# Modulation weights on another DMA queue, and scores of 512 queries in one bank: a diffusion layer on one core

## The chip, the core and the metric

The kernel runs on one core of one Trainium2 chip. Its engines work side by side, each through its own list of instructions in order: PE (TensorE, matmuls, with its weight loads shown as PEld), DVE (VectorE), ACT (ScalarE), POOL (GpSimd) and SP (SyncE). POOL and SP here do little but issue DMAs, each from a queue of its own. The metric is device time in microseconds of one execution, the median of three timed runs. Beside it stands one profiled execution, from which all durations of single instructions are taken.

## What is computed

One layer of a diffusion backbone in float32: 512 latent tokens and 256 context tokens of width 1024. Three parts follow each other: a SwiGLU network (FFN1), a pair of token mixers (retention and a convolution), and a second SwiGLU network. Each is modulated by vectors that come from a conditioning vector `c` times a large weight, `w_mod`.

```python
mods   = split(silu(c)     @ w_mod + b_mod, 9)          # shift, scale, gate for each of the three parts
mods_c = split(silu(c_ctx) @ w_mod + b_mod, 9)          # the same for the context tokens

h  = h  + 0.5 * g1  * swiglu(modulate(h,  n1, sh1,  sc1 ), w_ffn1_in, w_ffn1_out)
hc = hc + 0.5 * g1c * swiglu(modulate(hc, n1, sh1c, sc1c), w_ffn1_in, w_ffn1_out)

u, uc = modulate(h, nm, sh2, sc2), modulate(hc, nm, sh2c, sc2c)
q, k, v, rg, cv, ga, gb = split(u @ w_in)               # k and v of the context from uc
o = bidir_retention(rope(q), rope(k), v, decays, states of the context)     # 4 heads, 256 wide, values 512 wide
h = h + g2 * ((sigmoid(ga) * retention_branch(o, rg) + sigmoid(gb) * conv_branch(cv)) @ w_o)

h = h + 0.5 * g3 * swiglu(modulate(h, n2, sh3, sc3), w_ffn2_in, w_ffn2_out)
out = rmsnorm(h, final_norm)
```

For the retention, the kernel writes both directions and the context's state as one weighted product: the score of query n and key m is q.k times a decay that depends on n - m alone, over 512 latent and 256 context keys, and the output is the scores times the values.

## The kernel before

**Number format.** Each float32 operand of a matmul is split into a rounded high part and a low remainder (`split`, lines 320 and 321, or `unit`, lines 102 to 107: a DMA into `wraw`, the high part `wh` by ScalarE in line 104, the low part `wl` by VectorE in line 106). A product is then three matmuls (`mm3`, lines 113 to 115): high by high, high by low, low by high. The columns streamed by one matmul are at most 512, which fill one of the eight banks of the accumulator memory (`ps`, tag `ps`, 8 buffers).

**FFN1.** The 22 blocks of 128 hidden channels are worked off in six groups, `GROUPS1`. A group first forms its input products and then its output products. From the second group on, the input products of one block are a `chunk` (lines 414 to 470): seven block products in place of eight, each of 12 matmuls of 384 columns (line 439), with sums on VectorE before and after. A chunk loads two halves of `w1i` (lines 418 and 419, on SyncE) into `wraw`, which has four buffers: two chunks' worth. VectorE forms sums of the halves (425, 426, 429, 430), ScalarE and VectorE split them (393 and 394). Four accumulators are used for seven products: `pc` holds the fifth product, VectorE takes it off in line 453 (`p7 = p7 - pc`), and only then can the seventh product go into `pc`. So PE waits at that place for VectorE's line 453.

The output products of a group (`STEPS_OUT` loop) write partial sums to DRAM: `part_sum` scales the accumulator on ScalarE (666, 667) and adds it to `hdram` by an accumulating DMA that POOL issues (668).

**Modulation steps beside FFN1.** The later modulation vectors are formed while FFN1 runs, in 48 steps. A step (`mods`, lines 214 to 227) loads a 128x1024 block of `w_mod`, 512 KB, into a tile `wm`, of which there are two buffers (line 217), and multiplies and sums it on VectorE (226), once, or twice for vectors that the context needs too. So the load of step n must wait until the sum of step n - 2 has been taken. All 48 loads are issued by POOL (line 220). The steps are dealt out by `STEPS_OUT` = (8, 5, 5, 4, 4, 0) to the output products of the six groups and by `STEPS_IN` = (0, 5, 5, 4, 4, 4) to their input products, where `beside` calls `mod_step` (line 493). Counted from 0, steps 0 to 7 go with the first group's output products, 8 to 12 with the second group's input products, 13 to 17 with its output products, 18 to 22, 23 to 27, 28 to 31, 32 to 35, 36 to 39, 40 to 43 and 44 to 47 with the rest in turn. A step among output products also gets `past`, a column of the partial sum before: ScalarE copies it into the tile (line 219) ahead of the load, which keeps the load from going out before that partial sum is there.

**What sets the order.** The program is written as one sequence; a scheduler then lays out each engine's list ahead of time. At each point it takes, of the instructions that it expects to be able to run on that engine, the one that comes first in the program; what it expects comes from its own cost model. On the chip each list is run strictly in order, and an instruction that waits holds up all behind it on its engine or queue.

**Retention, one head** (`retention`, lines 811 to 967). Queries and keys are projected and rotated (`roped`), the context's keys projected (`keys_c`). Then, for two halves of 256 queries (`nh`, line 893): scores for three pairs of key blocks (each pair fills one bank with 2 x 256 columns, line 907), the decay by one VectorE product per pair (913, with the decays read from the strips `sx` and `sc` through `windows`, lines 786 to 789), a split (915) into tiles `gc0` to `gc5`. After the first half's scores come the values (`values`, 144 matmuls of 512 columns into six banks) and a convolution chunk, after the second half's scores the first two gates. Each half ends with the outputs of its two blocks of 128 queries (line 930, 18 matmuls each) and their normalisation (932 to 936).

Of the kernel before, what the change touches and what calls it, by code (L numbers as in the profile page):

```python
# [10 lines left out]
F32 = mybir.dt.float32  # L11
# [5 lines left out]
P = 128  # L17
# [47 lines left out]
def hybrid_layer_kernel(ctx: ExitStack, tc: tile.TileContext, a: dict, out: bass.AP):  # L65
# [23 lines left out]
    def ps(shape=(P, 512)):  # L89
        count[0] += 1  # L90
        return pp.tile(list(shape), F32, tag="ps", name=f"ps_{count[0]}")
# [119 lines left out]
        nc.vector.tensor_scalar(ab1[:, 1, b, v:v + 1], dots[:, b, v, 0:1], dots[:, b, v, 1:2],  # L211
                                vec[:, V_BM + b:V_BM + b + 1], ALU.add, ALU.add)

    def mods(n, past=None):

        i, b = MOD_STEPS[n]
        raw = t_((P, D), F32, "wm", 2)
        if past is not None:
            nc.scalar.copy(raw[:, 0:1], past)
        nc.gpsimd.dma_start(raw, a["w_mod"][n])  # L220
        j = 8 * i + b
        for v, dst in ((0, mx), (1, mc)):
            if v == 1 and i > 4:
                continue
            junk = tmp((P, D), BF16)
            nc.vector.scalar_tensor_tensor(  # L226
                junk, raw, 1.0, ccrow[v], ALU.mult, ALU.mult, accum_out=dst[:, j:j + 1])
# [244 lines left out]
    def ffn1(u):  # L472
        g = []

        def keep(j, s):
            hi, lo = t_((P, LA), F32R, f"hx{2 * j}"), t_((P, LA), F32R, f"hx{2 * j + 1}")
            split(hi, lo, s)
            g.append((hi, lo))

        def gate(s, c, pa, pb):  # L480
            nc.scalar.activation(s[:, c], pa, AF.Silu)
            nc.vector.tensor_mul(s[:, c], s[:, c], pb)

        ux, uc = part(u, xs), part(u, cx)
        todo_g = start(ux, uc, gate)

        nc.gpsimd.dma_start(hdram[:, 0, L - 1:L + 1], todo_g[0][:, L - 1:L + 1])
        nc.gpsimd.dma_start(hdram[:, :, xs], a["xT"])
        nc.gpsimd.dma_start(hdram[:, :, cx], a["ctxT"])
        off = 0  # L490
        for gi, (k0, nk) in enumerate(GROUPS1):
            steps = spread(STEPS_IN[gi], 2 * nk - 2)
            beside = lambda: mod_step(next(steps, 0))
            for j in range(2 if k0 == 0 else 0, nk):
                if k0 and j == nk - 1:
                    g.append((t_((P, LA), F32R, f"hx{2 * j}"), t_((P, LA), F32R, f"hx{2 * j + 1}")))
                    chunk(k0 + j, u, t, beside, lambda s, c: split(g[-1][0][:, c], g[-1][1][:, c], s[:, c]))
                elif k0:
                    keep(j, chunk(k0 + j, u, t, beside, None))
                    beside()  # L500
                if k0:
                    continue
                wa, wb = units(a["w1i"][j])
                pa, pb, pc = ps(), ps(), ps((P, 2, LC))
                proj(pa, wa, ux)
                proj(pb, wb, ux)
                proj(pc[:, 0, :], wa, uc)
                proj(pc[:, 1, :], wb, uc)
                if j == 2:
                    t = [operands(kb) for kb in range(4)]  # L510
                    for i, s in enumerate(todo_g):
                        keep(i, s)
                s = t_((P, LA), F32, "sg", 4)
                gate(s, xs, pa, pb)
                gate(s, cx, pc[:, 0, :], pc[:, 1, :])
                keep(j, s)
            n = 2 * nk * P
            last = k0 + nk == NJ
            gx_, gc_ = part(g, xs), part(g, cx)
            if last:  # L520
                h, hc = open_h()

            def out_units(mm):
                hi, lo = unit(a["w1o"][mm, :, off:off + n], n)
                return [(hi[:, i * n // 2:(i + 1) * n // 2], lo[:, i * n // 2:(i + 1) * n // 2]) for i in range(2)]

            steps = spread(STEPS_OUT[gi], 8)
            past = None
            for mm in () if last else range(4):
                w = out_units(mm)  # L530
                px, pc = [ps() for _ in range(2)], [ps() for _ in range(2)]
                for ks in (range(nk - 1), (nk - 1,)) if mm == 0 else (range(nk),):
                    for i in range(2):
                        proj(px[i], w[i], gx_, ks)
                        proj(pc[i][:, :LC], w[i], gc_, ks)
                for i in range(2):
                    mod_step(next(steps), past)
                    r = part_sum(2 * mm + i, px[i], pc[i][:, :LC])
                    past = r[:, 0:1] if k0 else None
            if last:  # L540

                w = [x for mm in range(4) for x in out_units(mm)]
                pc = [ps()[:, :LC] for _ in range(6)]
                for ks in (range(nk - 1), (nk - 1,)):
                    for i in range(6):
                        proj(pc[i], w[i], gc_, ks)
                        if ks[-1] == nk - 1:
                            evac1c(hc, i, pc[i])
                for i in (6, 7):
                    pc = ps()[:, :LC]  # L550
                    proj(pc, w[i], gc_)
                    evac1c(hc, i, pc)
                for i in range(4):
                    px = ps()
                    proj(px, w[i], gx_)
                    evac1(h, i, px, xs)
                    tail1(i - 4, h, hc)
                px = [ps() for _ in range(4)]
                for m, c in enumerate(HALVES):
                    for i in range(4):  # L560
                        proj(px[i][:, c], w[4 + i], gx_, c=c)
                        evac1(h, 4 + i, px[i][:, c], c)
                        tail1(4 * m + i, h, hc)
            off += n
            del g[:]
        return h
# [69 lines left out]
    def spread(total, slots):  # L636
        return (total * (i + 1) // slots - total * i // slots for i in range(slots))

    def mod_step(count, past=None):
        for _ in range(count):  # L640
            if todo:
                n = todo.pop(0)
                mods(n, past)
                if n < 8:
                    for key, src in (("x1", mx), ("c1", mc)):
                        nc.vector.tensor_scalar(hg[key][:, n:n + 1], src[:, 16 + n:17 + n],
# [136 lines left out]
        nc.vector.tensor_add(t1, t1, t2)  # L783
        split(hi, lo, t1)

    def windows(strip, off, n):

        w = strip[:, off:off + n]
        return bass.AP(w.tensor, w.offset, [list(w.ap[0]), [P, 2], [1, n]])

    def strips(hd):

        gf, gb = lg[:, hd:hd + 1], lg[:, 4 + hd:5 + hd]
# [17 lines left out]
    def retention(hd):  # L811
# [78 lines left out]
            gate.append((g, g[:, i % 2, :]))  # L890


        for nh in range(2):
            qs = slice(nh * 256, (nh + 1) * 256)
            pt = []
            for i in range(3):
                pq = ps((P, 2, 256))
                for jj in range(2):
                    mb = 2 * i + 1 - jj
                    for kb in range(2):  # L900
                        if mb < 4:
                            ks = slice(mb * P, (mb + 1) * P)
                            w = kh[:, kb, ks], kl[:, kb, ks]
                        else:
                            ks = slice((mb - 4) * P, (mb - 3) * P)
                            w = kch[:, kb, ks], kcl[:, kb, ks]
                        mm3(pq[:, jj, :], w, (q[kb][0][:, qs], q[kb][1][:, qs]), kb == 0, kb == 1)
                s = tmp((P, 2, 256))
                if i < 2:
                    dw = windows(sx, 384 - P * (2 * i + 1) + nh * 256, 256)  # L910
                else:
                    dw = windows(sc, nh * 256, 256)
                nc.vector.tensor_mul(s, pq, dw)
                hi, lo = t_((P, 2, 256), F32R, f"gc{i}"), t_((P, 2, 256), F32R, f"gc{3 + i}")
                split(hi, lo, s)
                pt.append((hi, lo))
            if nh == 0:
                values()
                conv_at(hd)
            else:  # L920
                wr = units(a["w_rg"][2 * hd])
                for i in range(2):
                    gates(i, wr[i])
            for nb in range(2):
                tb = 2 * nh + nb
                po = ps()
                for mb in range(6):
                    hi, lo = pt[mb // 2]
                    w = (hi[:, 1 - mb % 2, nb * P:(nb + 1) * P], lo[:, 1 - mb % 2, nb * P:(nb + 1) * P])
                    mm3(po, w, v[mb], mb == 0, mb == 5)  # L930
                bs = tmp((P, 16))
                nc.vector.bn_stats(bs[:, 0:6], po)
                nc.vector.bn_aggr(bs[:, 6:8], bs[:, 0:6])
                rsqrt(bs[:, 9:10], bs[:, 8:9], bs[:, 7:8], 1.0)
                o = t_((P, DV), F32, f"o{tb}")
                nc.vector.tensor_scalar(o, po, bs[:, 6:7], bs[:, 9:10], ALU.subtract, ALU.mult)
                on.append(o)
        r = []

        def gated(db):  # L940
# [267 lines left out]
```

## Time and profile before

| | |
|---|---|
| median of the timed runs | 1764.94 us |
| lowest and highest of three | 1762.32 and 1765.55 us |
| the profiled execution | 1768.33 us |
| its span | 1766.6 us |
| instructions | 22538 |
| granted TensorE clock over the span | 0.988 |
| loads of `wm` by POOL | 48, 512.0 KB each, 5.1 us to landing (median) |
| accumulating writes of `hdram` by POOL | 40, 384.0 KB each, 7.4 us |
| loads of `w1i` by SyncE | 44, 512.0 KB each, 4.8 us |

The span runs from the first to the last instruction; the profiled execution's own time is 1.7 us longer. In rows of the timeline the columns are start, duration, engine, line, operation, output and inputs with their shapes, and in brackets the idle time of the engine before it and what ended it. Matmuls overlap each other, so the distance from start to start tells what one costs, not its duration. A row of the waits names who waited for whom, then the sum in us, how many times, and the longest. A row of DMA issues gives the count, the size and the median time from issue to landing.

### The profile page before, as it was taken

What the parts mean: (1) busy time and instruction counts of PE and PEld (TensorE: products, weight loads), DVE (VectorE), ACT (ScalarE), POOL (GpSimd) and SP (SyncE); (2) the same over time, 40 slices, a digit from 0 to 9 for tenths busy, and PEclk for the clock granted to TensorE, in tenths of its full rate; (3) what the DMA queues carried; (4) which work ended last, traced back from release to release, by engine and by line L of the source; (5) the groups of instructions that cost most, each with busy time, mean ns of one, the idle gap of its engine ahead of it and who ended that gap; (6) DMA issues with size and microseconds to landing.
All of it is one profiled execution on the core that took longest, in us unless ns stands there. A gap on an engine that the chain in (4) does not pass through costs nothing. (4 is left out here: it accounts for less than half of the span.)

```text
span 1766.6 us, 22538 instructions
## 1 busy us (share of the span) xinstructions
PE 1724.1 (98%) x8947; PEld 1499.1 (85%) x8947; DVE 1146.1 (65%) x1831; ACT 672.1 (38%) x964; POOL 116.3 (7%) x208
## 2 busy tenths in 40 slices
PE   7899999998999999999999999999999999999997
PEld 4689999997999988888888888888888988888887
DVE  6895868575667898792985778393755644333335
ACT  4543444443434623342342433233563422222222
POOL 0011020201111100000000000001100000000000
PEclk9999999998999999999999999999999999999998
DMA  9267383847554321251151124215553244223221
GB/s 329 73 239 153 120 203 119 202 114 191 137 161 157 125 85 60 72 178 60 48 170 68 60 78 161 71 37 181 202 189 119 72 161 137 96 88 103 95 84 49
DMA packets 67999, 223.03 MB, mean 126 GB/s; under 512 B 8178, under 2 KB 9202, under 8 KB 67892
## 3 DMA queue, kind: packets, MB, share of 16 engines
q1 hardware_dynamic: 44928, 146.82, 24.8%
q0 software_dynamic: 22240, 73.69, 15.0%
q8 instruction: 70, 1.15, 0.3%
q10 hardware_dynamic: 724, 1.07, 0.2%
q14 instruction: 37, 0.30, 0.0%
HBM read 192.71 MB, written 31.98 MB: 127 GB/s over the span
## 5 line engine op out<-in xcount | busy, mean ns | idle before, releaser
L104 ACT CAST wh<-wraw 128x1024 fp32r<-128x1024 f32 (+2 forms) x212 | 219.7, 1037 | 558.1 <-PE ps L114 305.9
L106 DVE TENSOR_TENSOR wl<-wraw,wh 128x1024 fp32r<-128x1024 f32 (+2 forms) x212 | 254.7, 1203 | 200.6 <-ACT wh L104 195.7
L113 PE MATMUL ps<-uh,wh 128*128 128x512 f32 (+1 forms) x924 | 332.4, 363 | 2.5 <-ACT uh L576 1.7
L115 PE MATMUL ps<-uh,wl 128*128 128x512 f32 (+1 forms) x924 | 330.6, 359 | 0.7 <-DVE wl L106 0.7
L114 PE MATMUL ps<-ul,wh 128*128 128x512 f32 (+1 forms) x832 | 298.1, 359 | 0.0
L114 PE MATMUL ps<-gx,wh 128*128 128x512 f32 (+1 forms) x544 | 204.0, 377 | 0.0
L115 PE MATMUL ps<-gx,wl 128*128 128x512 f32 (+1 forms) x544 | 204.0, 377 | 0.0
L113 PE MATMUL ps<-gx,wh 128*128 128x512 f32 (+1 forms) x544 | 203.7, 377 | 0.2 <-ACT gx L320 0.2
L113 PEld LDWEIGHTS ps<-uh,wh 128*128 128x128 f32 x924 | 175.6, 191 | 30.6 <-ACT uh L576 3.1
L115 PEld LDWEIGHTS ps<-uh,wl 128*128 128x128 f32 x924 | 175.9, 191 | 26.3 <-DVE wl L106 1.1
L763 DVE SCALAR_TENSOR_TENSOR h<-y,vec,h 128x512 f32<-128x512 f32 x240 | 179.6, 749 | 5.5
L114 PEld LDWEIGHTS ps<-ul,wh 128*128 128x128 f32 x832 | 158.7, 191 | 23.5 <-issue 0.9
L114 PE MATMUL ps<-hx,wh 128*128 128x512 f32 (+1 forms) x368 | 121.9, 331 | 0.0
L113 PE MATMUL ps<-hx,wh 128*128 128x512 f32 (+1 forms) x368 | 121.8, 331 | 0.0
L115 PE MATMUL ps<-hx,wl 128*128 128x512 f32 (+1 forms) x368 | 121.6, 330 | 0.0
L113 PEld LDWEIGHTS ps<-gx,wh 128*128 128x128 f32 x544 | 102.1, 188 | 19.1 <-ACT gx L320 0.4
L114 PEld LDWEIGHTS ps<-gx,wh 128*128 128x128 f32 x544 | 102.0, 188 | 18.8
L115 PEld LDWEIGHTS ps<-gx,wl 128*128 128x128 f32 x544 | 102.0, 188 | 18.7
L226 DVE SCALAR_TENSOR_TENSOR t<-wm,kh 128x1024 bf16<-128x1024 f32 x48 | 58.3, 1222 | 59.7 <-DMA wm<-in_w_mod 59.5
L439 PE MATMUL ps<-th,wl 128*128 128x384 f32 x288 | 96.2, 334 | 0.0
L439 PE MATMUL ps<-th,wh 128*128 128x384 f32 x288 | 96.2, 334 | 0.0
L439 PE MATMUL ps<-tl,wh 128*128 128x384 f32 x288 | 96.2, 334 | 0.0
(286 smaller groups left out, 3088.2 us busy)
## 6 DMA issues: line engine op xcount, KB each, us to landing
wm<-in_w_mod POOLq DMA_DIRECT2D x48, 512.0 KB, 5.1
wraw<-in_w1i SPq DMA_DIRECT2D x44, 512.0 KB, 4.8
wraw<-in_w2i SPq DMA_DIRECT2D x44, 512.0 KB, 3.6
hdram<-sg POOLq DMA_DIRECT2D x40, 384.0 KB, 7.4
wraw<-in_w1o SPq DMA_DIRECT2D x16, 512.0 KB, 3.5
wraw<-in_w_cv SPq DMA_DIRECT2D x16, 512.0 KB, 3.6
wraw<-in_w_v SPq DMA_DIRECT2D x16, 512.0 KB, 6.4
wraw<-in_w_rg SPq DMA_DIRECT2D x16, 512.0 KB, 3.6
```

Of the source, the lines that this page charges most:

```text
L104: nc.scalar.copy(hi, raw)
L106: nc.vector.tensor_sub(lo, raw, f32(hi))
L113: nc.tensor.matmul(o, w[0], x[0], start=first, stop=False)
L114: nc.tensor.matmul(o, w[0], x[1], start=False, stop=False)
L115: nc.tensor.matmul(o, w[1], x[0], start=False, stop=last)
L226: nc.vector.scalar_tensor_tensor(junk, raw, 1.0, ccrow[v], ALU.mult, ALU.mult, accum_out=dst[:, j:j + 1])
L439: nc.tensor.matmul(o, w[i][:, ws], x[k][m], start=first and k == n == 0, stop=k == 3 and n == 2, skip_group_check=True)
L763: nc.vector.scalar_tensor_tensor(o, y[:, t:t + L], vec[:, w0 + t:w0 + t + 1], o, ALU.mult, ALU.add)
```

## The change

Two edits that have nothing to do with each other.

First, `mods` and `mod_step` take a queue. Where `beside` calls them among the input products of FFN1, the load goes to SyncE's queue; among the output products it stays on POOL's.

Second, the scores of a head are formed for all 512 queries at once: six key blocks, each with its own bank of 512 columns, one product with the decay strip each (so that `windows` is no longer needed), and tiles `gc0` to `gc5` for the high and `gc8` to `gc13` for the low parts. Values and the convolution chunk follow all six, then the four blocks of outputs, with the first two gates between the second and the third.

```diff
-    def mods(n, past=None):
+    def mods(n, past=None, queue=None):
...
-        nc.gpsimd.dma_start(raw, a["w_mod"][n])
+        (queue or nc.gpsimd).dma_start(raw, a["w_mod"][n])
...
-            beside = lambda: mod_step(next(steps, 0))
+            beside = lambda: mod_step(next(steps, 0), queue=nc.sync)
...
-    def mod_step(count, past=None):
+    def mod_step(count, past=None, queue=None):
...
-                mods(n, past)
+                mods(n, past, queue)
...
-        for nh in range(2):
-            qs = slice(nh * 256, (nh + 1) * 256)
-            pt = []
-            for i in range(3):
-                pq = ps((P, 2, 256))
-                for jj in range(2):
-                    mb = 2 * i + 1 - jj
-                    for kb in range(2):
...
-                        mm3(pq[:, jj, :], w, (q[kb][0][:, qs], q[kb][1][:, qs]), kb == 0, kb == 1)
-                s = tmp((P, 2, 256))
...
-                nc.vector.tensor_mul(s, pq, dw)
-                hi, lo = t_((P, 2, 256), F32R, f"gc{i}"), t_((P, 2, 256), F32R, f"gc{3 + i}")
-                split(hi, lo, s)
-                pt.append((hi, lo))
-            if nh == 0:
-                values()
-                conv_at(hd)
-            else:
+        pt = []
+        for mb in range(6):
+            pq = ps()
+            for kb in range(2):
...
+                mm3(pq, w, q[kb], kb == 0, kb == 1)
+            off = 384 - P * mb if mb < 4 else P * (5 - mb)
+            s = tmp()
+            nc.vector.tensor_mul(s, pq, (sx if mb < 4 else sc)[:, off:off + L])
+            hi, lo = t_((P, L), F32R, f"gc{mb}"), t_((P, L), F32R, f"gc{8 + mb}")
+            split(hi, lo, s)
+            pt.append((hi, lo))
+        values()
+        conv_at(hd)
+        for tb in range(4):
+            if tb == 2:
                 wr = units(a["w_rg"][2 * hd])
                 for i in range(2):
                     gates(i, wr[i])
-            for nb in range(2):
-                tb = 2 * nh + nb
-                po = ps()
...
+            po = ps()
+            for mb in range(6):
+                c = slice(tb * P, (tb + 1) * P)
+                mm3(po, (pt[mb][0][:, c], pt[mb][1][:, c]), v[mb], mb == 0, mb == 5)
```

More of the change, by code (lines that the diff above doesn't have):

```diff
@@ L784, in roped @@
         split(hi, lo, t1)
-    def windows(strip, off, n):
-        w = strip[:, off:off + n]
-        return bass.AP(w.tensor, w.offset, [list(w.ap[0]), [P, 2], [1, n]])
     def strips(hd):
@@ L890, in gates @@
             gate.append((g, g[:, i % 2, :]))
-        for nh in range(2):
-            qs = slice(nh * 256, (nh + 1) * 256)
-            pt = []
-            for i in range(3):
-                pq = ps((P, 2, 256))
-                for jj in range(2):
-                    mb = 2 * i + 1 - jj
-                    for kb in range(2):
-                        if mb < 4:
-                            ks = slice(mb * P, (mb + 1) * P)
-                            w = kh[:, kb, ks], kl[:, kb, ks]
-                        else:
-                            ks = slice((mb - 4) * P, (mb - 3) * P)
-                            w = kch[:, kb, ks], kcl[:, kb, ks]
-                        mm3(pq[:, jj, :], w, (q[kb][0][:, qs], q[kb][1][:, qs]), kb == 0, kb == 1)
-                s = tmp((P, 2, 256))
-                if i < 2:
-                    dw = windows(sx, 384 - P * (2 * i + 1) + nh * 256, 256)
-                else:
-                    dw = windows(sc, nh * 256, 256)
-                nc.vector.tensor_mul(s, pq, dw)
-                hi, lo = t_((P, 2, 256), F32R, f"gc{i}"), t_((P, 2, 256), F32R, f"gc{3 + i}")
-                split(hi, lo, s)
-                pt.append((hi, lo))
-            if nh == 0:
-                values()
-                conv_at(hd)
-            else:
+        pt = []
+        for mb in range(6):
+            pq = ps()
+            for kb in range(2):
+                if mb < 4:
+                    ks = slice(mb * P, (mb + 1) * P)
+                    w = kh[:, kb, ks], kl[:, kb, ks]
+                else:
+                    ks = slice((mb - 4) * P, (mb - 3) * P)
+                    w = kch[:, kb, ks], kcl[:, kb, ks]
+                mm3(pq, w, q[kb], kb == 0, kb == 1)
[9 more added lines that the diff above has]
+            if tb == 2:
                 wr = units(a["w_rg"][2 * hd])
@@ L923, in retention @@
                     gates(i, wr[i])
-            for nb in range(2):
-                tb = 2 * nh + nb
-                po = ps()
[L927 to L937, printed above, removed]
+            po = ps()
+            for mb in range(6):
+                c = slice(tb * P, (tb + 1) * P)
+                mm3(po, (pt[mb][0][:, c], pt[mb][1][:, c]), v[mb], mb == 0, mb == 5)
+            bs = tmp((P, 16))
+            nc.vector.bn_stats(bs[:, 0:6], po)
+            nc.vector.bn_aggr(bs[:, 6:8], bs[:, 0:6])
+            rsqrt(bs[:, 9:10], bs[:, 8:9], bs[:, 7:8], 1.0)
+            o = t_((P, DV), F32, f"o{tb}")
+            nc.vector.tensor_scalar(o, po, bs[:, 6:7], bs[:, 9:10], ALU.subtract, ALU.mult)
+            on.append(o)
         r = []
```

## The prediction

> **What bounds the kernel now.** First the page's head, then the view of the waits (us in total, times, longest), to see which engine is never idle and who makes it wait.
>
> ```profile
> span 1766.6 us, 22538 instructions
> PE 1724.1 (98%) x8947; PEld 1499.1 (85%) x8947; DVE 1146.1 (65%) x1831; ACT 672.1 (38%) x964; POOL 116.3 (7%) x208
> PE ps L439 <- DVE t L453: 11.7, 3, 7.4
> DVE t L226 <- DMA wm<-in_w_mod: 59.5, 23, 8.5
> ```
>
> PE is busy for 98%, so only matmul time or a wait of PE moves the end. Its largest wait is three stalls in the input products of FFN1 (L439), each ended by VectorE's subtraction L453. VectorE itself waits 59.5 us for modulation weights (L226, the multiply-sum). So the second step is the timeline of PE around the three stalls.
>
> ```profile
> 353.90 0.44 PE L439 MATMUL ps<-uh,wh 128*128 128x384 f32 x1 [0.64 <-DVE t L453]
> ...
> 422.93 0.34 PE L439 MATMUL ps<-th,wl 128*128 128x384 f32 x1
> 430.68 0.69 PE L439 MATMUL ps<-uh,wh 128*128 128x384 f32 x1 [7.42 <-DVE t L453]
> ...
> 436.61 0.39 PE L439 MATMUL ps<-uh,wh 128*128 128x384 f32 x1
> ...
> 500.72 0.33 PE L439 MATMUL ps<-tl,wh 128*128 128x384 f32 x1
> ...
> 502.45 0.34 PE L439 MATMUL ps<-th,wl 128*128 128x384 f32 x1
> 506.40 0.69 PE L439 MATMUL ps<-uh,wh 128*128 128x384 f32 x1 [3.61 <-DVE t L453]
> ...
> 511.68 0.40 PE L439 MATMUL ps<-ul,wh 128*128 128x384 f32 x1
> ```
>
> Ten matmuls pass between 500.72 and 502.45: 0.173 us from start to start. The next one was due at 423.10 and came at 430.68: 7.58 us late. The 18 after it took 5.93 us where 18 x 0.173 is 3.11, so the stall left PE slow for another 2.8. The second stall is 506.40 - 502.62 = 3.78, and its 16 slow matmuls add 5.28 - 2.77 = 2.5. The first, 353.90, costs some 0.8 and no slow stretch. Together 17.5 us, all that can be won here.
>
> Third step: why was VectorE late? Timelines of POOL, ScalarE and VectorE before 430, and the time to landing of the two loads (issues at 411.89 and 413.00, in that order).
>
> ```profile
> 405.61 0.86 POOL L668 DMA_DIRECT2D hdram<-sg  x1 [2.52 <-ACT sg L667]
> 411.89 0.58 POOL L220 DMA_DIRECT2D wm<-in_w_mod  x1 [5.43 <-DVE wl L394]
> ...
> 413.00 0.94 POOL L220 DMA_DIRECT2D wm<-in_w_mod  x1
> ...
> 424.28 0.56 POOL L220 DMA_DIRECT2D wm<-in_w_mod  x1 [9.45 <-DVE t L226]
> 407.27 0.19 ACT L219 COPY wm<-sg 128x1 f32<-128x1 f32 x1
> wm<-in_w_mod POOLq DMA_DIRECT2D x1, 512.0 KB, 4.5
> wm<-in_w_mod POOLq DMA_DIRECT2D x1, 512.0 KB, 9.7
> 409.87 1.23 DVE L226 SCALAR_TENSOR_TENSOR t<-wm,kh 128x1024 bf16<-128x1024 f32 x1 [3.75 <-DMA wm<-in_w_mod]
> ...
> 422.74 1.23 DVE L226 SCALAR_TENSOR_TENSOR t<-wm,kh 128x1024 bf16<-128x1024 f32 x1 [8.45 <-DMA wm<-in_w_mod]
> ...
> 427.79 1.22 DVE L226 SCALAR_TENSOR_TENSOR t<-wm,kh 128x1024 bf16<-128x1024 f32 x1 [1.53 <-DMA wm<-in_w_mod]
> ...
> 430.08 0.55 DVE L453 TENSOR_TENSOR t<-t,ps 128x384 f32<-128x384 f32 x1
> ```
>
> VectorE's wait to 422.74 ends with the load issued second (413.00 + 9.7). I number the steps as in the code: 32 to 35 belong to the output products of the fourth group, 36 to 39 to the input products after them. Step 35 has its `past` copy done at 407.46 (L219), yet POOL stands still until 411.89. What it waits for there is a slot freed by VectorE at 409.87 to 411.1, that of step 34, which step 36 takes. So I read the two issues as 36, then 35: a load of the input products, waiting for its slot at the head of POOL's queue, holds back an older load that VectorE wants first. The third stall has the same picture, `past` ready at 486.98:
>
> ```profile
> 486.79 0.19 ACT L219 COPY wm<-sg 128x1 f32<-128x1 f32 x1
> 490.63 0.56 POOL L220 DMA_DIRECT2D wm<-in_w_mod  x1 [4.64 <-DVE t L226]
> ...
> 491.72 0.90 POOL L220 DMA_DIRECT2D wm<-in_w_mod  x1
> 499.77 1.23 DVE L226 SCALAR_TENSOR_TENSOR t<-wm,kh 128x1024 bf16<-128x1024 f32 x1 [6.25 <-DMA wm<-in_w_mod]
> ...
> 505.80 0.55 DVE L453 TENSOR_TENSOR t<-t,ps 128x384 f32<-128x384 f32 x1
> ```
>
> **The change, part 1: 22 of 48 loads go from POOL to SyncE** (5+5+4+4+4; the 26 of the output products stay). Durations: loads on SyncE in this stage, the slowest kind of load there, and step 34's load on POOL among the accumulating writes (issued 401.65).
>
> ```profile
> wraw<-in_w1i SPq DMA_DIRECT2D x44, 512.0 KB, 4.8
> sg<-in_w_mod SPq DMA_DIRECT2D x8, 256.0 KB, 7.3
> wm<-in_w_mod POOLq DMA_DIRECT2D x1, 512.0 KB, 8.1
> 414.32 0.33 SPq L419 DMA_DIRECT2D wraw<-in_w1i  x1
> ```
>
> Second stall: with 36 gone, POOL issues 35 when the copy is done, 407.5; it lands 8.1 later, 415.6. Step 36 goes out on SyncE at about 411.3 and lands at 416.1, before VectorE wants it. Step 37 needs the slot of 35: free at 416.8, issued 417.0, landed 421.8. L453 came 2.29 after that multiply-sum began (427.79 to 430.08), so 424.1, and the matmul 0.6 later, 424.7: 1.6 late in place of 7.58. That saves 6.0, and the slow stretch of 2.8, since the 0.64 stall left none. Third stall: step 43 goes out at 487.0, lands at 495.1; L453 followed 6.03 later, 501.1, matmul 501.7, before the 502.6 at which it is due. Saves 3.78 + 2.5 = 6.3. The first stall I halve: 0.4. Sum 8.8 + 6.3 + 0.4 = **15.5**. Ends: with 9.7 on POOL and 7.3 on SyncE the second stall is still 5.7 with its slow stretch (saves 1.9) and the third 0.7 (saves 5.6), 7.5 in all; with all stalls gone 17.5.
>
> What SyncE's queue now carries: 22 issues of 0.33 us on an idle sequencer. What stands behind a moved load that waits are the `w1i` loads of later chunks. Group 12's third chunk has its second half issued at 414.32, landed by 419.4; a chunk is 84 x 0.173 = 14.5 us of PE, the first began at 423.1 - 72 x 0.173 = 410.6, so the third starts at 439.7 at the earliest. There are 20 us of cover, and both kinds of slot are freed by VectorE in its fixed order.
>
> **Part 2: scores.** 72 matmuls of 256 columns per head become 36 of 512: 288 to 144. Between the first two rows lie 36 of the old kind, between the last two 57 of 512.
>
> ```profile
> 637.30 0.28 PE L113 MATMUL ps<-gx,kh 128*128 128x256 f32 x1
> ...
> 641.62 0.40 PE L113 MATMUL ps<-wh,uh 128*128 128x512 f32 x1
> ...
> 654.56 0.39 PE L113 MATMUL ps<-wh,uh 128*128 128x512 f32 x1
> ...
> 943.00 0.39 PE L115 MATMUL ps<-gx,kl 128*128 128x256 f32 x1 [0.44 <-DVE kl L321]
> ...
> 794.44 0.68 DVE L913 TENSOR_TENSOR t<-ps,sc 128x512 f32<-128x512 f32 x1
> ...
> 803.41 1.23 DVE L106 TENSOR_TENSOR wl<-wraw,wh 128x1024 fp32r<-128x1024 f32 x1 [6.91 <-ACT wh L104]
> ```
>
> 4.32 / 36 = 0.120 and 12.94 / 57 = 0.227, so a pair saves 13 ns: 144 x 0.013 = **1.9**. [...] The third head's wait for `kl` (943.00) comes 0.5 later in the new order and loses about that. VectorE and ScalarE do the same number of products and splits (six of 512 elements per head), in one burst of six. Six of the eight banks are then held as the values start; their third bank is wanted 2 x 6 x 0.227 = 2.7 us after the scores end, while the first score bank has had 9.5 us. In the second head VectorE ends its last score product at 795.1 and then idles for 6.91: that covers the burst. Were it gone, a bank could cost up to 1.4 us per head, 5.6 in all. Part 2: 2.4, between -3.2 and 2.6. PE's waits in retention sum to under 1 us, so nothing else is hidden there.
>
> Sum: 15.5 + 2.4 = **17.9**. Against the profiled execution's own 1768.33 (1.7 around the span) that is 1750.4; against the median of the timed runs, 1764.94, it is 1747.0. The profiled run is 3.4 above the median, perhaps with longer stalls, so I take 1748.
>
> **Rivals.**
>
> One stall stays: VectorE's next wait, for step 37, keeps the second stall at 5.7. For it speaks that 37 cannot go out before 35 is consumed. 1764.9 - 1.9 - 5.6 - 2.4 = 1755.
>
> Only the scores count. If loads land late because all queues are full, not because one stands in another's way, 35 lands at 422 wherever 36 is queued: 1764.9 - 2.4 = 1762.5. For it: 9.7 us to land. Against it: 5.43 of POOL's standstill lie before the issue, and the first of the two landed in 4.5. [...]
>
> Slower: the order on VectorE is planned ahead from expected landings. If loads on SyncE are planned to land sooner, one more multiply-sum may be put ahead of L453 in each group, and VectorE then waits there for one more round, 4.8 + 1.2 = 6 us. It decides once that round ends after PE wants L453. Place and price: in the group of 353.90 the stall grows by 6 with a slow stretch of 2.5; in that of 430.68, 424.7 + 6 = 430.7, as before; in that of 506.40, 501.7 + 6 = 507.7, 1.3 more than before. 8.5 + 1.3 - 2.4 = +7.4: 1772. Against it: an extra load also needs one of two slots, which the sums before it must free.
>
> **Numbers.** Forecast 0.63 (1743 to 1754), one stall stays 0.15, only the scores 0.11, slower 0.11. 0.2% is 3.5 us, about what a measurement of this kernel can tell from no change; so faster 0.78, same 0.11, slower 0.11. The range runs from 1743 (all stalls gone, 20.1, and a little) to 1762: forecast, one stall, and the edge of the third case.
>
> **What would show it.** POOL issues the last load of each output stage right after its L219 copy; SyncE shows 22 L220 issues; no PE wait on L453 above 2 us, and no stretch of matmuls at twice 0.173 us in FFN1. Scores: 36 matmuls at 0.227 per head, and no wait of PE for a bank as the values start. It is wrong if VectorE's wait before L453 stays at 6 to 8 us, or if PE waits for `wh` of a chunk, which would be SyncE's queue held up.

## The result, and the profile after

| | before | after |
|---|---|---|
| median of the runs | 1765.26 us (6 runs) | 1755.0 us (6 runs) |
| lowest and highest | 1762.32 and 1768.85 | 1749.04 and 1755.77 |
| profiled execution, span | 1768.33, 1766.6 us | 1749.04, 1747.2 us |
| granted clock over the span | 0.988 | 0.995 |

The ratio is 0.9935, with a 95% interval of 0.992 to 0.995: 10.3 us faster, where 17 were forecast (1764.94 to 1748). The time lies inside the range (1743 to 1762), but 7 above the forecast and just outside the 1743 to 1754 that the prediction gave to it.

The profiled execution of after is the quickest of its six runs, that of before was 3 above its median. The two profiles differ by 19.4 us, then, and not all of that is the change. First the page's head and PE's waits in FFN1, as shown of before:

```profile
span 1747.2 us, 22268 instructions
PE 1712.2 (98%) x8803; PEld 1484.0 (85%) x8803; DVE 1145.2 (66%) x1831; ACT 671.5 (38%) x964; POOL 103.9 (6%) x186
```

```profile
PE ps L439 <- DVE t L453: 5.1, 2, 3.5
```

The 144 matmuls fewer are there, POOL has 22 issues fewer, and of three stalls on L453 (11.7 us) two are left (5.1). The timeline of PE shows which:

```profile
352.70 0.45 PE L439 MATMUL ps<-uh,wh 128*128 128x384 f32 x1 [1.59 <-DVE t L453]
...
421.72 0.34 PE L439 MATMUL ps<-th,wl 128*128 128x384 f32 x1
425.57 0.45 PE L439 MATMUL ps<-uh,wh 128*128 128x384 f32 x1 [3.50 <-DVE t L453]
425.85 0.34 PE L439 MATMUL ps<-ul,wh 128*128 128x384 f32 x1
426.03 0.35 PE L439 MATMUL ps<-uh,wl 128*128 128x384 f32 x1
```

The third stall is gone, the second is 3.68 late (425.57 - 421.72 - 0.17) in place of 7.58, and the first is longer: 1.59 in place of 0.64. In this execution no slow stretch follows the second stall (0.18 from start to start at once). Now what leads up to it, in the timelines of ScalarE, POOL, SyncE and VectorE:

```profile
406.06 0.19 ACT L219 COPY wm<-sg 128x1 f32<-128x1 f32 x1
...
406.55 0.56 POOL L220 DMA_DIRECT2D wm<-in_w_mod  x1 [1.27 <-ACT wm L219]
...
409.60 5.36 SPq L220 DMA_DIRECT2D wm<-in_w_mod  x2
...
413.37 1.22 DVE L226 SCALAR_TENSOR_TENSOR t<-wm,kh 128x1024 bf16<-128x1024 f32 x1 [1.74 <-DMA wm<-in_w_mod]
...
416.83 1.23 DVE L226 SCALAR_TENSOR_TENSOR t<-wm,kh 128x1024 bf16<-128x1024 f32 x1 [1.09 <-DMA wm<-in_w_mod]
...
420.09 1.23 DVE L226 SCALAR_TENSOR_TENSOR t<-wm,kh 128x1024 bf16<-128x1024 f32 x1 [2.02 <-DMA wm<-in_w_mod]
...
421.24 1.22 DVE L394 TENSOR_TENSOR wl<-wraw,wh 128x1024 fp32r<-128x1024 f32 x1
422.50 0.69 DVE L429 TENSOR_TENSOR wraw<-wy,wraw 128x512 f32<-128x512 f32 x1
423.22 0.69 DVE L430 TENSOR_TENSOR wraw<-wraw 128x512 f32<-128x512 f32 x1
423.83 1.22 DVE L394 TENSOR_TENSOR wl<-wraw,wh 128x1024 fp32r<-128x1024 f32 x1
424.97 0.55 DVE L453 TENSOR_TENSOR t<-t,ps 128x384 f32<-128x384 f32 x1
```

POOL issues step 35 right behind its copy, at 406.55, and it lands within 6.8 us (its sum starts at 413.37). Steps 36 and 37 are the two issues of SyncE. Their sums follow at 416.83 and 420.09. But between the sum of 37 and L453 there now stand four operations, so L453 comes 4.88 after that sum began; in before it came 2.29 after.

**Where the 19.4 us of the profiles lie.** The stages are cut at four rows of PE: the first and the last L439, and the first matmul behind the head loop (L986 before, L971 after).

```profile
155.90 0.34 PE L439 MATMUL ps<-uh,wh 128*128 128x384 f32 x1
...
554.56 0.33 PE L439 MATMUL ps<-uh,wl 128*128 128x384 f32 x1
...
1230.82 0.59 PE L986 MATMUL ps<-acc,ones 128*128 128x512 f32 x1
```

```profile
153.86 0.34 PE L439 MATMUL ps<-uh,wh 128*128 128x384 f32 x1
...
540.37 0.33 PE L439 MATMUL ps<-uh,wl 128*128 128x384 f32 x1
...
1212.50 1.02 PE L971 MATMUL ps<-acc,ones 128*128 128x512 f32 x2
```

Up to FFN1, whose code is the same, after is 2.04 quicker (155.90 - 153.86). FFN1 takes 386.51 in place of 398.66: 12.15. The mixers take 672.13 in place of 676.26: 4.13. The rest, again the same code, is 1.08 quicker (1766.6 - 1230.82 against 1747.2 - 1212.50). So 3.1 us come from code that the change doesn't touch. They are chance: in the profiles of all kernels here FFN1's first L439 starts between 153.05 (e10, all of whose loads are on POOL as in before) and 156.33 (e4). Of the 4.13 in the mixers, some 1.2 will turn out to be chance as well.

### The profile page after: what moved, and what is told of

Read it like the earlier page. It is cut to its first block, busy times and chain, and to the rows that moved or that the text cites. A ratio compares the mean times of both kernels' runs of the same rounds, so it can differ in the third digit from the quotient of the medians.

```text
span 1747.2 us, 22268 instructions
## 1 busy us (share of the span) xinstructions
PE 1712.2 (98%) x8803; PEld 1484.0 (85%) x8803; DVE 1145.2 (66%) x1831; ACT 671.5 (38%) x964; POOL 103.9 (6%) x186
## 5 line engine op out<-in xcount | busy, mean ns | idle before, releaser
L439 PE MATMUL ps<-th,wl 128*128 128x384 f32 x288 | 96.3, 334 | 0.0
L439 PE MATMUL ps<-th,wh 128*128 128x384 f32 x288 | 96.3, 334 | 0.0
L439 PE MATMUL ps<-tl,wh 128*128 128x384 f32 x288 | 96.3, 334 | 0.0
```

The lines of the kernel that those rows point to most:

```text
L439: nc.tensor.matmul(o, w[i][:, ws], x[k][m], start=first and k == n == 0, stop=k == 3 and n == 2, skip_group_check=True)
```

## The experiments

Two theories come first; others follow with the runs that test them. **Theory A**, the prediction's: steps 36 and 44 stood at the head of POOL's queue, waiting for a slot, ahead of 35 and 43, which VectorE wanted first. **Theory B**: it helps that 22 loads leave POOL's queue, whichever they are. The runs of before beside them had medians of 1765.93 (first four), 1765.59 (next four) and 1766.31 (last four).

| kernel | median, us | ratio to before, 95% interval |
|---|---|---|
| e1: the changed kernel again | 1753.93 | 0.9937 (0.9922 to 0.9952) |
| e2: queue only | 1757.11 | 0.9952 (0.9940 to 0.9964) |
| e3: scores only | 1764.36 | 0.9996 (0.9984 to 1.0008) |
| e4: scores, 36 and 44 on SyncE | 1753.85 | 0.9934 (0.9921 to 0.9947) |
| e5: all but 36 and 44 on SyncE | 1760.75 | 0.9974 (0.9958 to 0.9990) |
| e6: step 37 late | 1749.62 | 0.9914 (0.9891 to 0.9938) |
| e7: all steps late | 1754.85 | 0.9938 (0.9917 to 0.9959) |
| e8: queues exchanged | 1764.38 | 0.9989 (0.9971 to 1.0007) |
| e9: e5 again | 1762.80 | 0.9974 (0.9959 to 0.9989) |
| e10: e3 again | 1764.47 | 0.9991 (0.9976 to 1.0006) |
| e11: scores, 44 on SyncE | 1759.69 | 0.9956 (0.9940 to 0.9972) |
| e12: steps 29 and 37 late | 1746.61 | 0.9887 (0.9862 to 0.9912) |

### e1 to e3: the parts

e1 is the changed kernel without an edit. e2 is the kernel before with the diff's lines 214, 220, 493, 639 and 643 alone. e3 is the changed kernel with one line back:

```diff
-            beside = lambda: mod_step(next(steps, 0), queue=nc.sync)
+            beside = lambda: mod_step(next(steps, 0))
```

Expected of e1:

> The changed kernel once more, for a second profile of it beside parts of it. Both theories: 1755 (10 below before). Question: the profiled execution of the first run was 1749.0, 6 below the timed runs; its remaining stall of 3.7 us (the subtraction L453 in the group of 425.57) left no slow stretch behind it. Theory A (head of the queue: steps 36 and 44 no longer stand on POOL ahead of 35 and 43): if the profile shows that stall with 16 to 18 matmuls at about 0.33 us behind it, the span is 2 to 3 longer; the rest of the 6 must lie in the first 90 us, which ran 2.06 quicker in the first profile with the same code.

Expected of e2:

> The kernel before with the 22 loads on SyncE and the scores as before. Theory A and theory B alike: it has all of the gain but the scores' 2.4, so 1757.5 (8 below before). If the scores are worth nothing, 1755; if the burst of six scores costs something, below 1755.

Expected of e3:

> The scores in one bank, all loads on POOL as before. By the spacing of the matmuls 144 x 0.013 = 1.9, and 0.5 for the wait for kl: 1762.9 (2.4 below before), with the three stalls of FFN1 as before (11 to 12 us of waits on L453). If the 10.3 measured for the whole change comes from the queue alone, 1765.3.

e1 came out 12.0 below before; the first measurement gave 10.3. The second profile of the changed kernel has the same stall, and this time a slow stretch starts 1 us behind it:

```profile
426.31 0.44 PE L439 MATMUL ps<-uh,wh 128*128 128x384 f32 x1 [3.47 <-DVE t L453]
...
427.38 0.52 PE L439 MATMUL ps<-uh,wl 128*128 128x384 f32 x1
427.70 0.52 PE L439 MATMUL ps<-uh,wh 128*128 128x384 f32 x1
...
430.58 0.36 PE L439 MATMUL ps<-uh,wh 128*128 128x384 f32 x1
```

The first row is the end of the stall, the others show the stretch: from 427.38 to 430.58 PE starts 10 matmuls in 3.20 us, where 10 x 0.173 is 1.73, so 1.5 us are lost. FFN1 takes 388.82 here, by the same two rows as above.

The queue alone gains 8.8 us by the medians, the scores alone 1.6 (1.8 in e10), both together 12.0: as a sum, within what the intervals allow. The scores' part is too small for the timed runs, whose intervals for it (0.9976 to 1.0008) reach from 4 us faster to 1.4 slower. The trace of e3 has it: from 553.91 to 1227.65 the mixers take 673.74 in place of 676.26.

```profile
553.91 0.33 PE L439 MATMUL ps<-uh,wl 128*128 128x384 f32 x1
...
1227.65 0.59 PE L971 MATMUL ps<-acc,ones 128*128 128x512 f32 x1
```

So the scores are worth 2.52 where 2.4 were forecast, and the third head's wait for `kl` is no longer among PE's waits. The 4.13 of the first profile of after hold more, because a slow stretch at the start of retention, which before and e3 both have, is missing there; the last section shows its rows. In e3 no wait of PE for a bank as the values start is among its waits.

### e4, e11, e5 and e9: which loads

e4 puts only two steps on SyncE, e11 only step 44; e5 and e9 are the opposite of e4. In e4 and e11 line 493 is as before.

```diff
-        (queue or nc.gpsimd).dma_start(raw, a["w_mod"][n])
+        (nc.sync if n in (36, 44) else nc.gpsimd).dma_start(raw, a["w_mod"][n])     # e4; e11: n == 44
+        (nc.gpsimd if n in (36, 44) else queue or nc.gpsimd).dma_start(raw, a["w_mod"][n])     # e5, e9
```

Expected of e4:

> The change with only steps 36 and 44 on SyncE, the other 20 loads back on POOL. Theory A (only these two stand ahead of an older load at the head of POOL's queue where PE waits for it): the same as the whole change, 1755, with POOL issuing 35 and 43 right after their past copies and at most one stall of 3 to 4 us left. Theory B (what helps is that 22 loads leave POOL's crowded queue, or land sooner by SyncE): two of 22 do little, 1762, near the scores alone.

Expected of e11:

> The scores, and only step 44 on SyncE: the third stall by itself. By the prediction's term 6.3 below the scores alone: 1757 to 1758, with the stall of 7.5 left. If the first profiles are right that the slow stretch behind the third stall doesn't always come, less: 4 to 5 below, 1759.

Expected of e5:

> The changed kernel with steps 36 and 44 alone put back on POOL; the other 20 loads stay on SyncE. Theory A (those two stand at the head of POOL's queue ahead of 35 and 43): the stalls of 7.5 and 3.8 are back, 1764, as with the scores alone. Theory B (20 loads fewer in POOL's queue help by themselves): near the whole change, 1755.

Expected of e9, and of e10 beside it:

> Steps 36 and 44 back on POOL, 20 loads on SyncE, once more beside the scores alone on one chip (the first time it came out at 1760.8, between theory A's 1764 and theory B's 1755). Theory A: the two agree within 1.5 and both have stalls of 7 and 4 on L453. Theory B in part (the other 20 loads are worth 3 to 4 by themselves): this one is 3 to 4 below the scores alone, and a stall or a slow stretch is missing from its profile.

> The scores alone again, on one chip with the run before. By the spacing of the matmuls 2.4 below the kernel before, 1763.2; first time it was 1764.4.

Two of 22 loads give the whole gain: e4 and e1 agree within 0.1 us on one chip. The timeline of e4's POOL has step 35 go out soon after its copy of 407.84, and PE keeps the stall of the changed kernel, here with a slow stretch from its first matmul on (18 matmuls up to the last row):

```profile
408.82 0.58 POOL L220 DMA_DIRECT2D wm<-in_w_mod  x1 [1.78 <-ACT sg L667]
...
427.80 0.69 PE L439 MATMUL ps<-uh,wh 128*128 128x384 f32 x1 [3.96 <-DVE t L453]
...
433.68 0.34 PE L439 MATMUL ps<-uh,wh 128*128 128x384 f32 x1
```

With the two back on POOL, and only with them, POOL has the two issues together again, 3.8 behind the copy of 406.27, and VectorE waits 6.31 (timelines of e9):

```profile
410.06 0.56 POOL L220 DMA_DIRECT2D wm<-in_w_mod  x1 [4.58 <-DVE t L226]
...
411.16 0.91 POOL L220 DMA_DIRECT2D wm<-in_w_mod  x1
...
419.27 1.23 DVE L226 SCALAR_TENSOR_TENSOR t<-wm,kh 128x1024 bf16<-128x1024 f32 x1 [6.31 <-DMA wm<-in_w_mod]
```

That is theory A, by an addition and by an omission. Theory B keeps a remainder: over 24 runs each, e5 and e9 have a mean of 1762.1 and e3 and e10 of 1764.7, with standard errors of 0.6; on the one chip that ran both, e9 is 1.8 below e10 in the means, with a standard error of 1.1. So the other 20 loads seem to be worth some 2 us while 36 and 44 stay on POOL. Once these two have left, no difference shows in six runs each (e4 against e1). The traces don't show where the 2 us lie: the second stall is 6.96 and 4.93 in e5 and e9 against 7.62 and 7.40 in e3 and e10, but the first and the third are longer there, and FFN1 takes 398.93 and 396.86 against 398.63 and 398.19. Why, no run here tells.

e11 gives the third stall by itself: it is gone, and the second is left at 6.41. In the medians e11 is 4.8 below e10, in the means 5.4 with a standard error of 1.2, so the 6.3 of the prediction's term is not ruled out. Step 36 adds the rest, some 5 to 6 us (e11 to e4, on two chips).

### e8: the queues exchanged

```diff
-        (queue or nc.gpsimd).dma_start(raw, a["w_mod"][n])
+        (nc.gpsimd if queue else nc.sync if n >= 8 else nc.gpsimd).dma_start(raw, a["w_mod"][n])
```

> The changed kernel with the two queues exchanged: loads of the input products on POOL, those of the output products on SyncE (from step 8 on). Theory A (what counts is that a load of the input products and one of the output products do not share a queue): 35 and 43 go out when their copies are done, 1755, as the whole change. Theory F (it must be SyncE that carries the loads of the input products): a load that waits at the head of POOL's queue now holds back the accumulating writes, one that waits on SyncE holds back weights of chunks; 1762 or more, with PE waiting for wh or the writes late.

1764.38, no clear difference from before: theory A as I put it there failed. It isn't enough that the two kinds of load don't share a queue. The profiled execution is the slowest of the 12 (1769.76). Its waits of SyncE's queue from 400 to 412, and the timelines of SyncE and VectorE:

```profile
SPq L418 <- DVE wl L394: 10.8, 1, 10.8
411.67 0.33 SPq L418 DMA_DIRECT2D wraw<-in_w1i  x1
412.09 1.39 SPq L220 DMA_DIRECT2D wm<-in_w_mod  x2
...
419.72 1.22 DVE L226 SCALAR_TENSOR_TENSOR t<-wm,kh 128x1024 bf16<-128x1024 f32 x1 [7.48 <-DMA wm<-in_w_mod]
```

Counted through, the sum at 419.72 is that of step 34. ScalarE's copy for it starts at 406.59, but its load goes out only at 412.09: ahead of it in SyncE's queue stands a chunk's weights, the `w1i` load of 411.67, which waits 10.8 us for a slot of its own. VectorE then waits 7.48 for step 34, the steps behind it are late too, and PE's second stall is 8.5. So it is the same fault with another culprit: now a chunk's weights stand ahead. Theory F has the time, but only part of its mechanism: in FFN1, PE waits for L453 and once, 0.6 us, for ScalarE (L445), never for `wh`. What these runs support is the narrower form: nothing that waits for a later event may stand ahead of a load that is wanted sooner.

### e6, e7 and e12: what is left of the gain

**Theory C**: what is left of the second stall is VectorE's order; the sum of step 37 and the operations behind it stand ahead of L453. **Rival D**: L453 itself waits for something late. e6 makes step 37 start after that L453, by a copy of one column of its result. On PE nothing changes its place. On VectorE that sum does, and behind L453 two operations (L462 and an L394) exchange places; ScalarE has the one copy more:

```diff
-        nc.vector.tensor_sub(p7, p7, pc)
+        nc.vector.tensor_sub(p7, p7, pc); held[:] = [p7[:, 0:1]]
...
-            beside = lambda: mod_step(next(steps, 0), queue=nc.sync)
+            beside = lambda: mod_step(next(steps, 0), held[0] if todo[:1] == [37] else None, nc.sync)
```

> The changed kernel, with step 37 made to start after the subtraction L453 of the chunk whose stall is left (its load and its sum come later, all else in the same order on each engine). Theory C (what is left of the second stall, 3.5 to 4.0, is the sum of step 37 standing ahead of L453 in VectorE's order, with its wait of 2 for the load): L453 follows the sum of 36 by four operations of 3.8 in all, the stall shrinks from 3.5 or 4.0 to about 1 and can leave no slow stretch, so 4 to 5 below the changed kernel: 1749 to 1750. Rival D (L453 waits for a product or a weight that is late itself): the stall stays, 1754.

1749.62, 4.3 below e1 (the runs of before beside the two differ by 0.3; the two intervals against before just overlap). The timelines of VectorE and PE:

```profile
417.46 1.23 DVE L226 SCALAR_TENSOR_TENSOR t<-wm,kh 128x1024 bf16<-128x1024 f32 x1 [0.95 <-DMA wm<-in_w_mod]
...
422.33 0.55 DVE L453 TENSOR_TENSOR t<-t,ps 128x384 f32<-128x384 f32 x1
...
422.27 0.34 PE L439 MATMUL ps<-th,wl 128*128 128x384 f32 x1
422.93 0.45 PE L439 MATMUL ps<-uh,wh 128*128 128x384 f32 x1 [0.33 <-DVE t L453]
```

L453 comes 4.87 after the sum of 36: the same four operations stand between, but that sum is early. The stall falls to 0.33, with no slow stretch: theory C, and rival D is out.

e7 applies this to every step of the input products: the first of a chunk's pair depends on the chunk's L453, the second on the chunk's product.

```diff
-        beside()
...
         nc.vector.tensor_sub(p7, p7, pc)
+        beside(p7[:, 0:1])
...
-                    keep(j, chunk(k0 + j, u, t, beside, None))
-                    beside()
+                    s = chunk(k0 + j, u, t, beside, None)
+                    keep(j, s), beside(s[:, 0:1])
```

> The changed kernel with every step of the input products made to start after a subtraction L453 (the first step of a chunk's pair) or after the chunk's product (the second). Theory C: no stall of PE on L453 left in any group, 1748. Rival E: sums put off hold the two slots longer, steps of the output products are late next, and new stalls cost as much as they save: 1755 or more.

1754.85: the time of rival E, and its reason. The edit takes out a line ahead of the subtraction, which is L452 in this kernel. PE's waits in FFN1, then the timelines of PE and VectorE:

```profile
PE ps L439 <- DVE wl L394: 3.2, 5, 1.1
PE ps L439 <- DVE t L452: 2.2, 1, 2.2
359.15 0.44 PE L439 MATMUL ps<-uh,wh 128*128 128x384 f32 x1 [2.16 <-DVE t L452]
352.54 1.22 DVE L226 SCALAR_TENSOR_TENSOR t<-wm,kh 128x1024 bf16<-128x1024 f32 x1 [1.69 <-DMA wm<-in_w_mod]
...
358.55 0.55 DVE L452 TENSOR_TENSOR t<-t,ps 128x384 f32<-128x384 f32 x1
```

So theory C's "no stall left in any group" failed: one wait for the subtraction is left, 2.16 in the group of the first stall, and a slow stretch of 1.6 follows it. The sum at 352.54 is that of step 27, a step of the output products; in e1 it starts at 341.80. It is late, as rival E has it, and the subtraction comes 6.0 behind it. The five other waits are for the low parts of weights (L394); ahead of the two longest, sums that were put off stand in VectorE's list. e12 goes back to single steps: 37, and 29, which stands in the same place ahead of the first stall.

```diff
-            beside = lambda: mod_step(next(steps, 0), queue=nc.sync)
+            beside = lambda: mod_step(next(steps, 0), held[0] if todo[:1] in ([29], [37]) else None, nc.sync)
```

> Step 37 late as before, and step 29 too, which stands in the same place ahead of L453 in the group of the first stall (1.6 to 1.8). Theory C: that stall goes as well, 1748. Rival E: the sums put off lie ahead of the next chunk's operations instead (in VectorE's order three of them now stand together ahead of the next L453), a stall there takes its place: 1750 or more.

1746.61 in four runs, the best of all: 19.7 below before by the medians, its interval (0.9862 to 0.9912) clear of the changed kernel's, though not of e6's. Of PE's waits on L453 two are left, 0.5 us together; the longer one in its timeline:

```profile
420.95 0.44 PE L439 MATMUL ps<-uh,wh 128*128 128x384 f32 x1 [0.29 <-DVE t L453]
```

FFN1 takes 381.96 (154.25 to 536.21), 16.7 less than before. With the prediction's 17.5 for all three stalls that closes the account of this stage.

## Why the prediction was right or wrong

**The reading of POOL's queue: right.** Step 36 ahead of 35, and 44 ahead of 43, were the fault: these two loads alone give the gain (e4), and putting them back loses most of it (e5, e9). Step 35 was to go out when its copy is done, and did: copy at 406.06, issue at 406.55. Step 36 was to land within 4.8 us, before VectorE wants it; from SyncE at 409.60 it took 7.2, and that cost little, since the sum of 36 waited 1.09. SyncE has 22 such issues, as foretold, and in FFN1 of after PE waits for no chunk's weights, so the cover of 20 us held. (The chunk that the prediction places in group 12 belongs to the group that starts at block 15; the sum is not touched by that.)

**The third stall, 6.3: right in kind.** It is gone in every kernel with 44 alone or all 22 loads on SyncE. Alone it measured 4.8 (5.4 in the means) in the timed runs.

**The second stall, 8.8: the step that failed.** The prediction has "L453 came 2.29 after that multiply-sum began (427.79 to 430.08), so 424.1". This carries VectorE's order of before over into the new kernel. The list is laid out anew: L429, L430 and one more L394 came ahead of L453 (in before, L429 and L430 follow it, at 431.15 and 431.87), which makes it 4.88. Against the moment at which PE wants the product, L453 was forecast 1.0 late (424.1 - 423.10) and came 3.08 late (424.97 - 421.89); 2.08 more. The new order costs 2.59 (4.88 - 2.29), and 0.5 of it came back, because the sum of 37 began that much sooner against that moment. The trace of before had a row to warn of it, in the group of the first stall:

```profile
348.42 1.23 DVE L226 SCALAR_TENSOR_TENSOR t<-wm,kh 128x1024 bf16<-128x1024 f32 x1 [1.31 <-DMA wm<-in_w_mod]
...
353.30 0.55 DVE L453 TENSOR_TENSOR t<-t,ps 128x384 f32<-128x384 f32 x1
```

There L453 came 4.88 after the sum. With it the forecast would have been 421.8 + 4.9 + 0.6 = 427.3, a stall of 4.2.

**The slow stretch, 2.8: the same step's second half.** A stall of 1.6 was to leave none, and that part held: stalls of 1.59 to 1.80 on L453 left none. But the second stall, now 3.5 to 4.1, left none once, 1.5 us once (e1), and in e4 18 matmuls in 5.88 us (427.80 to 433.68), 2.8 lost. Before, stall and stretch were 10.4 together, so the term of 8.8 came out at 6.7, 5.2 and 3.5 in these three traces.

**The first stall, 0.4 gained: wrong in sign.** It grew from 0.64 to 1.59 in after and 1.80 in e1, and stayed at 0.60 in e4, where its loads are on POOL. The order is the same in all four (L453 4.88 after the sum of step 29). What grew is the time from the sum of 28 to that of 29: 2.54 in before and 2.39 in e4, 3.40 in after and 3.17 in e1, and step 29's load, issued on SyncE at 342.07 in after, is summed 5.2 us later, where in before, issued on POOL at 344.32, it was 4.1. e12 removes the stall by moving the sum of 29 behind L453.

**Scores, 2.4: right,** 2.52 in the trace of e3, while the timed runs are too coarse to tell it from nothing. In after the 36 score matmuls of the first head take 8.16 us (621.81 to 629.97), 0.227 from start to start, as in the rows of before. No wait of PE shows that the burst of six scores costs anything.

**The sum.** FFN1 gained 12.15, 9.84 and 9.34 in after, e1 and e4 where 15.5 was forecast; with 2.5 for the scores that is 11.8 to 14.7 in profiles, and 10.3 and 12.0 in medians. Against 17.9, 3 to 6 us lack in the profiles and 6 to 8 in the medians. e6 and e12 find them: 4.3, and 3.0 more by the medians, both by taking a sum out of the place ahead of L453.

**The rivals.** "One stall stays" gave 1755, the time that came, in part by luck: it let the second stall save only 1.9, where 3.5 to 6.7 were saved, and had no growth of the first. Its mechanism was near: VectorE waits for step 37. But the wait of 2.02 is the smaller half; it keeps the stall at 3.5 to 4.0, not 5.7. That the profiled execution of after (1749.04) comes near the forecast of 1748 is luck too: it is the quickest of its six. The rival on the slower side named the right danger, an order planned anew, with the wrong content: not one more sum ahead of L453 but three more operations. "Only the scores" is out (e4).

## What to carry to other kernels

A load that waits for its buffer at the head of a queue holds back the load behind it: in before, steps 35 and 43 went out 5.5 and 4.7 us after their copies were done (407.46 to 413.00, 486.98 to 491.72), in after 0.3 (406.25 to 406.55 for step 35). Look for issues that come out of a queue in pairs, the first released by a buffer and the second ready long before, and give the one that waits another queue, where nothing urgent stands behind it. A forecast that moves one instruction must not carry the old distances between others over: where a scheduler lays out the lists, take the worst distance that the trace shows between the two, not the one next to the stall. When a large wait is gone, look at what stands between the next landing and the instruction that PE waits for: taking one multiply-sum out of that place was worth 4.3 us, doing it to all of them gave that gain back.

## What the runs showed of the chip that was not expected

In these profiles the length of a stall, up to some 3.5 us, doesn't decide whether PE runs slow behind it. All 15 waits on L453 of 3.61 us and more gave a slow stretch (behind the 3.96 of e4, matmuls 0.32 from start to start in place of 0.173). Waits of 3.47 and 3.50 us gave one in one execution and none in the other. In e7 a wait of 2.16 gave one, which started 1 us later; in e5 a wait of 2.65 gave none. And a wait of 1.84 us at the start of retention, the same in both, left PE slow in before and not in after (the timeline of PE, before first):

```profile
603.23 0.70 PE L289 MATMUL ps<-t,ones 128*128 128x256 f32 x2 [1.84 <-DVE t L282]
...
604.24 0.41 PE L113 MATMUL ps<-uh,wh 128*128 128x256 f32 x1
604.45 0.41 PE L114 MATMUL ps<-ul,wh 128*128 128x256 f32 x1
```

```profile
588.96 0.70 PE L289 MATMUL ps<-t,ones 128*128 128x256 f32 x2 [1.84 <-DVE t L282]
...
589.73 0.28 PE L115 MATMUL ps<-uh,wl 128*128 128x256 f32 x1
589.85 0.28 PE L113 MATMUL ps<-uh,wh 128*128 128x256 f32 x1
```

From start to start it is 0.21 in the first and 0.12 in the second. Of the 14 profiles, all with a wait of 1.83 or 1.84 there, 7 have this stretch; it costs some 1.2 us (673.74 for the mixers in e3, which has it, against 672.51 in e1, which hasn't, with the same scores). What decides between the two, no trace here shows. For a forecast it means that behind a short stall a slow stretch is a chance, of 1.2 to 2.8 us here, and no fixed price.
